# A mixture of softmaxes on one core: one queue for loads and stores, prior read once, last two batches loaded by head

## The chip, the cores and the metric

The kernel runs on one core of one Trainium2 chip. The metric is the device time of one execution in microseconds (us). The profile of one execution has a span about 2 us shorter than the timed value (795.2 against 797.5 us for the kernel before); times quoted "in the span" are from its start. Engines: DVE is the vector engine, ACT the scalar engine, POOL is GpSimd, SP the sync engine, which here only issues DMAs.

## The reference

```
logits (32, 128, 4, 4096) float32, prior (32, 128, 4) float32
p = softmax(prior, last axis)          s = softmax(logits, last axis)
out[b, q, :] = sum over h of p[b, q, h] * s[b, q, h, :]      # (32, 128, 4096) float32
```

The 32 batches are independent. For a batch the 128 positions lie on the 128 partitions; a batch's logits are 8.4 MB, its output 2.1 MB.

## The kernel before

```
lpool bufs=2   # 64 KB per partition each: one batch of logits
epool bufs=4   # bfloat16 exps, 8 KB each
apool bufs=2   # float32 accumulators, 16 KB each
for b in range(B):
    nc.sync.dma_start(out=prior_t, in_=prior[b])             # 128 rows of 16 bytes
    nc.scalar.activation(ep, prior_t, AF.Exp, accum_out=psum)
    nc.vector.reciprocal(rpsum, psum)
    ltile = lpool.tile([P, H, V], FP32, name="ltile")
    if not last:
        nc.sync.dma_start(out=ltile, in_=logits[b])
    acc = apool.tile([P, V], FP32, name="acc")
    for h in range(H):
        ...                     # the last batch is loaded by head, its last head by quarters
        nc.scalar.activation(etile, ltile[:, h], AF.Exp, accum_out=dsum)
        ...                     # coeff = ep[:, h] * rpsum / dsum
        # h == 0: acc = etile * coeff, else: acc = etile * coeff + acc; the very last by quarters
    if not last:
        nc.gpsimd.dma_start(out=out[b], in_=acc)
```

Loads are issued by SP and stores by GpSimd, so they stand in two queues. Below, "load b" and "store b" are the DMAs of batch b, counted from 0. The accumulator of batch b is the one that batch b-2 used: its first accumulation has to wait until store b-2 has landed.

The softmax here doesn't subtract the row's maximum and nothing guards it: scores larger than these inputs give would overflow.

## Time and profile before

| quantity | value | where |
|---|---|---|
| time | 797.48 us (796.5 to 797.49, 3 runs) | runs |
| DVE, ACT busy | 70%, 59% of the span | page |
| DMA busy | 9 tenths or more in 38 of 40 slices | page |
| 64 KB load packet, 16 KB store packet | 2.42 us, 0.611 us | packet records of the trace |
| packets of one DMA engine in sum | 781.7 us | packet records |

A packet is one record of the trace: a piece of a transfer that one DMA engine moves, here 64 KB of a whole load or 16 KB of a store. A transfer has landed when all its completion counts are in.

From the page of the kernel before: the busy time of the engines, the busy share of the DMA engines in 40 slices (in tenths), and the two queues with packets, megabytes and share of 16 engines' span.

```profile
...
DVE 557.5 (70%) x420; ACT 472.1 (59%) x327; POOL 21.1 (3%) x39
...
DMA  9999999999999999999999999999999999999984
...
q1 hardware_dynamic: 10080, 268.51, 78.5%
q0 software_dynamic: 5040, 67.11, 19.8%
...
```

The two queues fill the DMA engines to 98%. The large packets of both run at 27 B/ns; 16 engines of that rate move 432 GB/s. Nobody else is near its limit.

Groups of instructions of the kernel before (line, engine, operation, shapes, count, then busy us in total and mean ns of one, then idle time before them and what ended it), and the DMA issues of prior (count, size each, us from issue to landing).

```profile
...
L78 ACT ACTIVATE etile<-ltile 128x4096 bf16<-128x4096 f32 x127 | 457.6, 3604 | 305.3 <-DMA ltile<-in_logits_dram 305.3
L107 DVE SCALAR_TENSOR_TENSOR acc<-etile,coeff,acc 128x4096 f32<-128x4096 bf16 x95 | 426.1, 4485 | 3.4
...
L105 DVE TENSOR_SCALAR acc<-etile,coeff 128x4096 f32<-128x4096 bf16 x32 | 75.3, 2353 | 1.1
...
prior_t<-in_prior_dram SPq DMA_DIRECT2D x32, 2.0 KB, 34.1
...
```

ACT needs 3.6 us for a head, DVE 2.35 us for the first head of a batch and 4.49 for each other one (SCALAR_TENSOR_TENSOR, "STT" in the prediction). Both fit well into the 24.2 us that the DMA engines need for one batch. ACT's idle time, 305 us, is waiting for loads.

The timeline of the tail (start us, duration us, engine, line, operation, operands; in brackets the idle time before).

```profile
...
746.45 0.53 POOL L116 DMA_DIRECT2D out_dram<-acc  x1 [23.06 <-DVE acc L107]
748.85 3.62 ACT L78 ACTIVATE etile<-ltile 128x4096 bf16<-128x4096 f32 x1 [10.14 <-DMA ltile<-in_logits_dram]
...
753.10 2.35 DVE L105 TENSOR_SCALAR acc<-etile,coeff 128x4096 f32<-128x4096 bf16 x1
...
771.29 2.65 POOL L116 DMA_DIRECT2D out_dram<-acc  x1 [24.31 <-DVE rden L82]
771.48 2.34 DVE L105 TENSOR_SCALAR acc<-etile,coeff 128x4096 f32<-128x4096 bf16 x1
...
789.02 0.53 POOL L103 DMA_DIRECT2D out_dram<-acc  x1 [0.67 <-DVE acc L95]
```

Load 30 lands at 748.7 us, batch 30's first accumulation is at 753.10, batch 31's at 771.48, and DVE works through without a pause of note. It has no idle time before the line at 771.48: store 29, issued at 746.45 in the other queue, was long out of the way.

The issue of load 2, and the window of the start (stretch, its length, then busy us of DVE, ACT and POOL, clock, DMA share, GB/s):

```profile
...
37.58 0.33 SPq L50 DMA_DIRECT2D ltile<-in_logits_dram  x1
...
```

```profile
...
38.00:46.00 8.00, 7.16 (x5) 3.14 (x1) 0.49 (x1) 1.00 0.92 393
...
```

### The profile page before, as it was taken

To read this page: it belongs to the slowest core of one execution; us is meant where nothing else is said; L and a number is where in the kernel's file an instruction comes from. 1 tells how busy PE (TensorE), PEld (TensorE's weight loads), DVE (VectorE), ACT (ScalarE), POOL (GpSimd) and SP (SyncE) were. 2 spreads that over 40 slices of the span, in tenths; PEclk is the share of its full clock that TensorE was granted. 3 is DMA by queue.
4 is the path that set the end of the run, shared out by engine and by line. 5 is a ranking of instruction groups with operands and counts; after the bars stand their busy time and mean duration, and the time that the engine had idled before them with its cause. 6 is when DMAs were issued, how large, how long until landed. Compare 5 with 4: busy or idle time off the path is not lost.

```text
span 795.2 us, 1113 instructions
## 1 busy us (share of the span) xinstructions
DVE 557.5 (70%) x420; ACT 472.1 (59%) x327; POOL 21.1 (3%) x39
## 2 busy tenths in 40 slices
DVE  0686678666687666786666876667866668766696
ACT  0776456765547755567655477545676555775491
POOL 0000000000000000000000000000000000000011
DMA  9999999999999999999999999999999999999984
GB/s 383 452 409 434 406 444 422 437 454 407 452 419 439 439 422 456 401 455 410 450 416 444 445 412 457 404 454 411 458 420 418 457 411 459 407 441 451 401 342 185
DMA packets 15131, 335.70 MB, mean 422 GB/s; under 512 B 5777, under 2 KB 5777, under 8 KB 6801
## 3 DMA queue, kind: packets, MB, share of 16 engines
q1 hardware_dynamic: 10080, 268.51, 78.5%
q0 software_dynamic: 5040, 67.11, 19.8%
q14 instruction: 11, 0.08, 0.0%
HBM read 268.50 MB, written 67.11 MB: 422 GB/s over the span
## 4 chain that ended last, share of the span: by engine, by line
DMA 66%; ACT 22%; issue 7%; DVE 4%; DVEq 0%; ACTq 0%; POOLq 0%; SPq 0%; POOL 0%
DMA ltile<-in_logits_dram 66%; ACT etile L78 22%; DVE acc L107 3%; DVE acc L95 0%; DVE acc L105 0%; DVE coeff L84 0%; DVEq L142 0%; ACTq L78 0%; DVE rden L82 0%; POOLq L142 0%; ACT ep L44 0%; SPq L41 0%; POOL out_dram L103 0%; DVE dsum L75 0%; DVE rpsum L46 0%
## 5 line engine op out<-in xcount | busy, mean ns | idle before, releaser
L78 ACT ACTIVATE etile<-ltile 128x4096 bf16<-128x4096 f32 x127 | 457.6, 3604 | 305.3 <-DMA ltile<-in_logits_dram 305.3
L107 DVE SCALAR_TENSOR_TENSOR acc<-etile,coeff,acc 128x4096 f32<-128x4096 bf16 x95 | 426.1, 4485 | 3.4
L82 DVE RECIPROCAL rden<-dsum 128x1 f32<-128x1 f32 x128 | 20.4, 160 | 220.6 <-ACT etile L78 220.6
L105 DVE TENSOR_SCALAR acc<-etile,coeff 128x4096 f32<-128x4096 bf16 x32 | 75.3, 2353 | 1.1
L116 POOL DMA_DIRECT2D out_dram<-acc x31 | 18.7, 604 | 754.8 <-DVE acc L107 730.5
L84 DVE TENSOR_SCALAR coeff<-ep,rpsum,rden 128x1 f32<-128x1 f32 x128 | 34.9, 273 | 3.5
L78 ACT ACTIVATION_READ_ACCUMULATOR etile<-ltile 128x1 f32 x127 | 23.7, 186 | 0.0
L46 DVE RECIPROCAL rpsum<-psum 128x1 f32<-128x1 f32 x32 | 4.6, 145 | 2.7 <-ACT ep L44 2.7
L44 ACT ACTIVATE ep<-prior_t 128x4 f32<-128x4 f32 x32 | 6.1, 189 | 0.4 <-DMA prior_t<-in_prior_dram 0.4
L44 ACT ACTIVATION_READ_ACCUMULATOR ep<-prior_t 128x1 f32 x32 | 6.0, 187 | 0.0
L95 DVE SCALAR_TENSOR_TENSOR acc<-etile,coeff,acc 128x1024 f32<-128x1024 bf16 x4 | 4.9, 1281 | 0.0
L68 ACT ACTIVATE etile<-ltile 128x1024 bf16<-128x1024 f32 x4 | 4.2, 1042 | 0.0
L103 POOL DMA_DIRECT2D out_dram<-acc x4 | 2.1, 532 | 13.5 <-DVE acc L95 13.5
L44 ACT ACT_TABLE_LOAD x1 | 1.3, 1283 | 0.7 <-PEq L131 0.7
L68 ACT ACTIVATION_READ_ACCUMULATOR etile<-ltile 128x1 f32 x4 | 0.8, 189 | 0.0
L75 DVE TENSOR_REDUCE dsum<-denom 128x1 f32<-128x4 f32 x1 | 0.1, 150 | 0.0
L131 POOL MEMSET const-float32-0.0<- 128x1 f32 x1 | 0.1, 98 | 0.2 <-issue 0.2
L131 POOL MEMSET const-bfloat16-1.0<- 128x1 bf16 x1 | 0.1, 101 | 0.0
L131 POOL MEMSET const-uint8-127<- 128x1 uint8 x1 | 0.1, 99 | 0.0
L131 POOL MEMSET const-float32-1.0<- 128x1 f32 x1 | 0.1, 98 | 0.0
## 6 DMA issues: line engine op xcount, KB each, us to landing
out_dram<-acc POOLq DMA_DIRECT2D x31, 2048.0 KB, 26.1
ltile<-in_logits_dram SPq DMA_DIRECT2D x3, 2048.0 KB, 24.5
ltile<-in_logits_dram SPq DMA_DIRECT2D x4, 512.0 KB, 30.0
out_dram<-acc POOLq DMA_DIRECT2D x4, 512.0 KB, 3.5
prior_t<-in_prior_dram SPq DMA_DIRECT2D x32, 2.0 KB, 34.1
ltile<-in_logits_dram SPq DMA_DIRECT2D x31, 34.4
```

The costliest lines, as they stand in the source:

```text
L44: nc.scalar.activation(ep, prior_t, AF.Exp, accum_out=psum)
L46: nc.vector.reciprocal(rpsum, psum)
L68: nc.scalar.activation(etile[:, c * CW : (c + 1) * CW], ltile[:, h, c * CW : (c + 1) * CW], AF.Exp, accum_out=denom[:, c : c + 1],)
L78: nc.scalar.activation(etile, ltile[:, h], AF.Exp, accum_out=dsum)
L82: nc.vector.reciprocal(rden, dsum)
L84: nc.vector.tensor_scalar(out=coeff, in0=ep[:, h : h + 1], scalar1=rpsum, scalar2=rden, op0=ALU.mult, op1=ALU.mult,)
L95: nc.vector.scalar_tensor_tensor(out=acc[:, cs], in0=etile[:, cs], scalar=coeff, in1=acc[:, cs], op0=ALU.mult, op1=ALU.add,)
L103: nc.gpsimd.dma_start(out=out[b, :, cs], in_=acc[:, cs])
L105: nc.vector.tensor_scalar_mul(out=acc, in0=etile, scalar1=coeff)
L107: nc.vector.scalar_tensor_tensor(out=acc, in0=etile, scalar=coeff, in1=acc, op0=ALU.mult, op1=ALU.add,)
L116: nc.gpsimd.dma_start(out=out[b], in_=acc)
L131: nc = _bacc.Bacc("TRN2", target_bir_lowering=False, num_devices=1)
```

## The change

The intent: take the small packets of prior out of the DMA stream, put loads and stores into one hardware queue in an order fixed by the program, and have the last two batches computed head by head as they arrive. Cut to its core:

```diff
-    epool bufs=4   (bfloat16)
+    epool bufs=2   (float32, the same bytes)
+    def pieces(b):
+        return 1 if b >= B - 2 else H          # heads per load
+    load(0)
+    nc.sync.dma_start(out=pr, in_=prior)       # [32 batches, 128 positions, 4 heads]
+    load(1)
+    ...       # softmax of prior on 32 partitions, 16 transposes of 32x32 to pp[128, H, B]
     for b in range(B):
-        nc.sync.dma_start(out=prior_t, in_=prior[b])
-        nc.scalar.activation(ep, prior_t, AF.Exp, accum_out=psum)
...
+                store(b - 1)       # last batch, last head: the store of batch 30
+                for c in range(NCHUNK):
+                    ...            # accumulate a quarter; after each second one:
+                        store(b, (c - 1) * CW, (c + 1) * CW)
-        if not last:
-            nc.gpsimd.dma_start(out=out[b], in_=acc)
+        if b + 2 < B:
+            load(b + 2)                        # SP
+        if not last and b < B - 2:
+            store(b)                           # SP, after the load
```

The order in the queue is thus load 2, store 0, load 3, store 1, and at the end load 30 (4 pieces), store 28, load 31 (4 pieces), store 29, store 30, two halves of store 31.

More of the change, by code (lines that the diff above doesn't have):

```diff
@@ L9 @@
 FP32 = mybir.dt.float32
-BF16 = mybir.dt.bfloat16
 AF = mybir.ActivationFunctionType
 ALU = mybir.AluOpType
+AX = mybir.AxisListType
 @with_exitstack
@@ L27, with load, store @@
     P = 128
-    assert S == P
+    assert S == P and B == 32
     lpool = ctx.enter_context(tc.tile_pool(name="lpool", bufs=2))
-    epool = ctx.enter_context(tc.tile_pool(name="epool", bufs=4))
+    epool = ctx.enter_context(tc.tile_pool(name="epool", bufs=2))
     apool = ctx.enter_context(tc.tile_pool(name="apool", bufs=2))
     spool = ctx.enter_context(tc.tile_pool(name="spool", bufs=8))
+    cpool = ctx.enter_context(tc.tile_pool(name="cpool", bufs=1))
+    def pieces(b):
+        return 1 if b >= B - 2 else H
+    ltiles = {}
+    def load(b):
+        lt = lpool.tile([P, H, V], FP32, name="ltile")
+        n = pieces(b)
+        for h in range(0, H, n):
+            nc.sync.dma_start(out=lt[:, h : h + n], in_=logits[b, :, h : h + n, :])
+        ltiles[b] = lt
+    accs = {}
+    def store(b, lo=0, hi=V):
+        nc.sync.dma_start(out=out[b, :, lo:hi], in_=accs[b][:, lo:hi])
+    load(0)
+    pr = cpool.tile([B, S, H], FP32, name="pr")
+    nc.sync.dma_start(out=pr, in_=prior)
+    load(1)
+    pmax = cpool.tile([B, S], FP32, name="pmax")
+    nc.vector.reduce_max(pmax, pr, axis=AX.X)
+    pc = cpool.tile([B, S, H], FP32, name="pc")
+    nc.vector.tensor_sub(pc, pr, pmax.unsqueeze(2).to_broadcast([B, S, H]))
+    pe = cpool.tile([B, S, H], FP32, name="pe")
+    nc.scalar.activation(pe, pc, AF.Exp)
+    psum = cpool.tile([B, S], FP32, name="psum")
+    nc.vector.reduce_sum(psum, pe, axis=AX.X)
+    prec = cpool.tile([B, S], FP32, name="prec")
+    nc.vector.reciprocal(prec, psum)
+    pn = cpool.tile([B, H, S], FP32, name="pn")
+    nc.vector.tensor_mul(
+        pn.rearrange("b h s -> b s h"), pe, prec.unsqueeze(2).to_broadcast([B, S, H])
+    )
+    pp = cpool.tile([P, H, B], FP32, name="pp")
+    for t in range(S // 32):
+        for h in range(H):
+            nc.vector.transpose(
+                pp[32 * t : 32 * (t + 1), h, :], pn[:, h, 32 * t : 32 * (t + 1)]
+            )
     NCHUNK = 4
@@ L39 @@
         last = b == B - 1
-        prior_t = spool.tile([P, H], FP32, name="prior_t")
-        nc.sync.dma_start(out=prior_t, in_=prior[b])
-        ep = spool.tile([P, H], FP32, name="ep")
-        psum = spool.tile([P, 1], FP32, name="psum")
-        nc.scalar.activation(ep, prior_t, AF.Exp, accum_out=psum)
-        rpsum = spool.tile([P, 1], FP32, name="rpsum")
-        nc.vector.reciprocal(rpsum, psum)
-        ltile = lpool.tile([P, H, V], FP32, name="ltile")
-        if not last:
-            nc.sync.dma_start(out=ltile, in_=logits[b])
+        lt = ltiles.pop(b)
@@ L52 @@
         acc = apool.tile([P, V], FP32, name="acc")
+        accs[b] = acc
         for h in range(H):
-            if last:
-                if h < H - 1:
-                    nc.sync.dma_start(out=ltile[:, h], in_=logits[b, :, h, :])
-                else:
-                    for c in range(NCHUNK):
-                        nc.sync.dma_start(
-                            out=ltile[:, h, c * CW : (c + 1) * CW],
-                            in_=logits[b, :, h, c * CW : (c + 1) * CW],
-                        )
@@ L64 @@
-            etile = epool.tile([P, V], BF16, name="etile")
-            denom = spool.tile([P, NCHUNK], FP32, name="denom")
-            if last and h == H - 1:
-                for c in range(NCHUNK):
-                    nc.scalar.activation(
-                        etile[:, c * CW : (c + 1) * CW],
-                        ltile[:, h, c * CW : (c + 1) * CW],
-                        AF.Exp,
-                        accum_out=denom[:, c : c + 1],
-                    )
-                dsum = spool.tile([P, 1], FP32, name="dsum")
-                nc.vector.reduce_sum(dsum, denom, axis=mybir.AxisListType.X)
-            else:
-                dsum = spool.tile([P, 1], FP32, name="dsum")
-                nc.scalar.activation(
-                    etile, ltile[:, h], AF.Exp, accum_out=dsum
-                )
+            split = last and h == H - 1
@@ L81 @@
+            et = epool.tile([P, V], FP32, name="etile")
+            dsum = spool.tile([P, 1], FP32, name="dsum")
+            nc.scalar.activation(et, lt[:, h], AF.Exp, accum_out=dsum)
+            coeff = spool.tile([P, 1], FP32, name="coeff")
             rden = spool.tile([P, 1], FP32, name="rden")
             nc.vector.reciprocal(rden, dsum)
-            coeff = spool.tile([P, 1], FP32, name="coeff")
-            nc.vector.tensor_scalar(
-                out=coeff,
-                in0=ep[:, h : h + 1],
-                scalar1=rpsum,
-                scalar2=rden,
-                op0=ALU.mult,
-                op1=ALU.mult,
-            )
@@ L92 @@
-            if last and h == H - 1:
+            nc.vector.tensor_mul(coeff, rden, pp[:, h, b : b + 1])
+            if h == 0:
+                nc.vector.tensor_scalar_mul(out=acc, in0=et, scalar1=coeff)
+            elif not split:
+                nc.vector.scalar_tensor_tensor(
+                    out=acc, in0=et, scalar=coeff, in1=acc, op0=ALU.mult, op1=ALU.add
+                )
+            else:
+                store(b - 1)
                 for c in range(NCHUNK):
@@ L95 @@
                     nc.vector.scalar_tensor_tensor(
-                        out=acc[:, cs],
-                        in0=etile[:, cs],
-                        scalar=coeff,
-                        in1=acc[:, cs],
-                        op0=ALU.mult,
-                        op1=ALU.add,
-                    )
-                    nc.gpsimd.dma_start(out=out[b, :, cs], in_=acc[:, cs])
-            elif h == 0:
-                nc.vector.tensor_scalar_mul(out=acc, in0=etile, scalar1=coeff)
-            else:
-                nc.vector.scalar_tensor_tensor(
-                    out=acc,
-                    in0=etile,
-                    scalar=coeff,
-                    in1=acc,
-                    op0=ALU.mult,
-                    op1=ALU.add,
-                )
-        if not last:
-            nc.gpsimd.dma_start(out=out[b], in_=acc)
+                        out=acc[:, cs], in0=et[:, cs], scalar=coeff, in1=acc[:, cs],
+                        op0=ALU.mult, op1=ALU.add,
+                    )
+                    if c % 2:
+                        store(b, (c - 1) * CW, (c + 1) * CW)
[3 more added lines that the diff above has]
+            store(b)
 _INS = ['logits', 'prior']
```

## The prediction

> **What bounds the kernel now.** The 16 DMA engines, by bytes. The page shows DMA at 9 tenths in 38 of 40 slices, 422 GB/s over the span; DVE is busy 70%, ACT 59%. In the trace's packets a 64 KB load packet takes 2.42 us and a 16 KB store packet 0.611 us: 27 B/ns for loads and stores, alone or mixed. From 3 to 770 us the engines' packets leave no idle time. They sum to 781.6 us per engine, a little overlapped; idle are 2.3 us at the start and about 14 us at the tail. The Trainium skill ("DMA: Bandwidth & Descriptors", section "Issuing engines are not separate DMA queues") says that all issuers share these engines; the trace agrees. One queue instead of two moves no byte faster.
>
> **What the change does.**
> 1. Prior: 4096 packets of 16 B at 9 ns (2.3 us per engine) become 32 rows of 2 KB (about 0.2 us). Fewer DMAs and larger tail pieces save perhaps 0.8 us; the first load starts 0.45 us earlier. All on the critical path: about -3.5 us.
> 2. Float32 exps change no duration (ACT 3.6 us per 4096; STT 4.49; TENSOR_SCALAR 2.35, where the Trainium skill "VectorE: DVE Perf Modes", tier table, gives float32 the 2x mode that this duration shows). Two exp buffers instead of four tie ACT to DVE two heads behind, so a batch's last exp comes about 3 us later: slack in the steady state (the next load is issued some 10 us before its turn).
> 3. Start: prior lands behind load 0 (22.6 us); then a chain of about 7 us (max, sub, exp behind the first large exp, sum, reciprocal, product, 16 transposes) delays the first accumulation. With two exp buffers batch 0's last exp ends near 43 us; load 2 waits for it, while load 1 is through at 40.7. A DMA gap: +3 us.
> 4. Tail, the decisive part. In one queue, store 29 stands behind load 31. Batch 31 accumulates into the buffer that store 29 reads, so its first DVE operation waits until about 6.5 us after load 31 has gone through, though its data came by head. Then DVE needs 2.35 + 3 x 4.9 us and the last half store 2.4 us: the end comes about 30 us after load 31's last packets. Before, it was 22 us, since store 29 shared the engines with load 31. The loads end earlier, at about 765.5 instead of 773, as two stores (9.7 us) now come after them. So the tail gives back what the order saved.
>
> **Sum.** Packets up to load 31 about 760.7 us (loads 621, stores 0 to 28 141.9, less the overlap), start 1.75, gap 3.2, tail 30.4: a span of 796 us against 795.2. Timed: 798 us, range 793 to 804. Faster by over 2% 0.03, within 2% 0.93, slower 0.04.
>
> **What the profile would show.** DMA 9 tenths but for a dip near 41-44 us and an emptier last 25 us; load packets still 2.42 us; DVE's first accumulation of each batch waiting for the store two batches back (about 6 us after the landing, harmless in the middle); batch 31's TENSOR_SCALAR waiting for store 29; the chain's end on DVE and a store; DVE busy near 550 us; 16 transposes under 3 us.
>
> **What would make it wrong.** Idle time at each change from load to store within one queue (64 changes: 0.1 us each is 6 us); a slower packet rate for stores from the hardware queue; batch 31's accumulation not waiting for store 29: then the end comes near 784 us, and without a start gap 781, the limit of "faster".

## The result, and the profile after

800.94 us median (800.46 to 801.67, 4 runs) against 797.49 us (796.5 to 797.68, 4 runs) in the same rounds. The ratio is 1.0051, with a 95% interval of 1.0035 to 1.0067: slower by half a per cent, within the band that counts as the same, and inside the predicted range. All ratios here are the mean time of one kernel's fast runs over the mean of the other's in the same rounds, so they are not quite the ratio of the medians. The kernel before had medians from 795.94 to 797.49 us in four sessions; experiments are therefore compared with each other by their ratios to it, and a difference of two ratios is put into us by multiplying with 797. The intervals of two ratios together leave such a difference uncertain by about 0.002, or 1.6 us.

The same parts of the page of the changed kernel:

```profile
...
DVE 547.0 (68%) x408; ACT 473.1 (59%) x258; POOL 0.2 (0%) x4
...
DMA  9989999999999999999999999999999999999992
...
q1 hardware_dynamic: 10272, 335.61, 97.7%
...
```

One queue now holds all bytes and fills the engines to 97.7%. The last digit of the DMA row has fallen from 4 to 2, and the third is no longer a 9: the engines are idle at the end and once near the start.

The groups of the changed kernel, and the issue of prior:

```profile
...
L94 ACT ACTIVATE etile<-ltile 128x4096 f32<-128x4096 f32 x128 | 462.4, 3613 | 314.1 <-DMA ltile<-in_logits_dram 250.4
L102 DVE SCALAR_TENSOR_TENSOR acc<-etile,coeff,acc 128x4096 f32<-128x4096 f32 x95 | 426.0, 4484 | 3.4
...
L100 DVE TENSOR_SCALAR acc<-etile,coeff 128x4096 f32<-128x4096 f32 x32 | 75.3, 2353 | 29.0 <-DMA out_dram<-acc 29.0
...
pr<-in_prior_dram SPq DMA_DIRECT2D x1, 64.0 KB, 22.0
```

Durations are those of before: float32 exps cost ACT 3.613 instead of 3.604 us and DVE nothing. The Trainium skill, "VectorE: DVE Perf Modes", the perf-mode tier table, gives `tensor_scalar` with float32 the 2x mode. The trace agrees: 4096 elements took 2353 ns, against 4484 ns for SCALAR_TENSOR_TENSOR, and the bfloat16 input before had taken the same 2353 ns. What is new is the end of the TENSOR_SCALAR line: 29.0 us of idle time that a store ended.

**The start.** The window and the issue of load 2 by SP:

```profile
...
38.00:46.00 8.00, 7.86 (x7) 6.06 (x5) 0.00 (x0) 1.00 0.69 262
...
```

```profile
...
43.00 0.33 SPq L45 DMA_DIRECT2D ltile<-in_logits_dram  x1
...
```

The DMA share in this window is 0.69 against 0.92. The packet records give 2.57 us of idle time per DMA engine between 38 and 50 us, and none there before. Load 1 was through, and load 2 was issued only at 43.00 us (before: 37.58). The timeline before it:

```profile
...
23.23 0.67 DVE L60 TENSOR_REDUCE pmax<-pr 32x128 f32<-32x512 f32 x1 [23.23 <-DMA pr<-in_prior_dram]
...
30.04 1.96 DVE L78 STREAM_TRANSPOSE pp<-pn 32x32 f32<-32x32 f32 x16
...
32.23 2.35 DVE L100 TENSOR_SCALAR acc<-etile,coeff 128x4096 f32<-128x4096 f32 x1
...
39.26 3.62 ACT L94 ACTIVATE etile<-ltile 128x4096 f32<-128x4096 f32 x1 [0.87 <-DVE rden L97]
...
```

Prior landed behind load 0, at 23.2 us; its softmax and 16 transposes (1.96 us) were done at 32.0; the first accumulation ran at 32.23. Batch 0's last exp started at 39.26 us, when an exp buffer was free, and load 2 waits for it.

**The tail.** The timeline, and the chain of waits that ended last (start us, us, what):

```profile
...
752.85 2.35 DVE L100 TENSOR_SCALAR acc<-etile,coeff 128x4096 f32<-128x4096 f32 x1 [3.20 <-DMA out_dram<-acc]
...
769.38 3.62 ACT L94 ACTIVATE etile<-ltile 128x4096 f32<-128x4096 f32 x1 [1.08 <-issue]
...
777.23 2.35 DVE L100 TENSOR_SCALAR acc<-etile,coeff 128x4096 f32<-128x4096 f32 x1 [3.75 <-DMA out_dram<-acc]
...
789.19 4.87 DVE L109 SCALAR_TENSOR_TENSOR acc<-etile,coeff,acc 128x1024 f32<-128x1024 f32 x4
```

```profile
...
745.49 31.71 DMA out_dram<-acc
...
777.23 2.36 DVE acc L100
...
```

The list of waits of the changed kernel (us in total, times, longest us):

```profile
...
DVE acc L100 <- DMA out_dram<-acc: 29.0, 30, 3.8
...
```

Load 31's last piece landed at 772.3 us. Two of batch 31's four exps were done by 772.9 us (the second is the line at 769.38); the other two wait for exp buffers, and those for DVE. DVE's first accumulation of batch 31 started at 777.23 us, 0.03 us after store 29 had landed (777.20). Batch 30's (the line at 752.85) had waited for store 28 in the same way. From 777.23 us on it is DVE to 794.1 us and the last half store, which landed at 798.05.

Landings of the last DMAs, from the completion counts in the trace (16 counts per DMA, read here as one from each engine: while those of store 30 come in, from 777.1 to 782.0 us, the packets in flight fall from 10 to none; "lag" is the time from the first to the last count):

```
changed kernel:  load 31 heads 0..3  757.7 762.6 767.5 772.3   lag 5.0
                 store 29 777.2  store 30 782.0  (lag 5.0)   halves of 31: 795.6 798.0  (lag 0.2)
kernel before:   load 31, its four last quarters  769.6 770.8 772.1 773.5   lag 3.1 to 3.3
```

More than one engine is late. Of the 16 counts of load 31's last piece, nine come within 0.7 us and the other seven spread over the rest in the changed kernel; in the kernel before 13 come within 0.7 us and three later.

### The profile page after: what moved, and what is told of

It reads as the page before. It is cut to its first block, busy times and chain, and to the rows that moved or that the text cites. A ratio compares the mean times of both kernels' runs of the same rounds, so it can differ in the third digit from the quotient of the medians.

```text
span 798.9 us, 996 instructions
## 1 busy us (share of the span) xinstructions
DVE 547.0 (68%) x408; ACT 473.1 (59%) x258; POOL 0.2 (0%) x4
## 3 DMA queue, kind: packets, MB, share of 16 engines
q1 hardware_dynamic: 10272, 335.61, 97.7%
## 4 chain that ended last, share of the span: by engine, by line
DMA 63%; DVE 16%; ACT 13%; issue 6%; DVEq 0%; ACTq 0%
DMA ltile<-in_logits_dram 56%; DVE acc L102 13%; ACT etile L94 13%; DMA out_dram<-acc 8%; DVE acc L100 1%; DVE rden L97 1%; DVE coeff L98 1%; DVE acc L109 0%; DVE pp L78 0%; DVEq L144 0%; DVE pn L71 0%; DVE prec L68 0%; DVE psum L66 0%; ACT pe L64 0%; ACTq L94 0%
## 5 line engine op out<-in xcount | busy, mean ns | idle before, releaser
L94 ACT ACTIVATE etile<-ltile 128x4096 f32<-128x4096 f32 x128 | 462.4, 3613 | 314.1 <-DMA ltile<-in_logits_dram 250.4
L102 DVE SCALAR_TENSOR_TENSOR acc<-etile,coeff,acc 128x4096 f32<-128x4096 f32 x95 | 426.0, 4484 | 3.4
L100 DVE TENSOR_SCALAR acc<-etile,coeff 128x4096 f32<-128x4096 f32 x32 | 75.3, 2353 | 29.0 <-DMA out_dram<-acc 29.0
L98 DVE TENSOR_TENSOR coeff<-rden,pp 128x1 f32<-128x1 f32 x128 | 20.4, 159 | 4.4
L60 DVE TENSOR_REDUCE pmax<-pr 32x128 f32<-32x512 f32 x1 | 0.7, 673 | 23.2 <-DMA pr<-in_prior_dram 23.2
L109 DVE SCALAR_TENSOR_TENSOR acc<-etile,coeff,acc 128x1024 f32<-128x1024 f32 x4 | 4.9, 1281 | 0.0
L78 DVE STREAM_TRANSPOSE pp<-pn 32x32 f32<-32x32 f32 x16 | 1.9, 169 | 0.1
```

The lines of the kernel that those rows point to most:

```text
L60: nc.vector.reduce_max(pmax, pr, axis=AX.X)
L78: nc.vector.transpose(pp[32 * t : 32 * (t + 1), h, :], pn[:, h, 32 * t : 32 * (t + 1)])
L94: nc.scalar.activation(et, lt[:, h], AF.Exp, accum_out=dsum)
L98: nc.vector.tensor_mul(coeff, rden, pp[:, h, b : b + 1])
L100: nc.vector.tensor_scalar_mul(out=acc, in0=et, scalar1=coeff)
L102: nc.vector.scalar_tensor_tensor(out=acc, in0=et, scalar=coeff, in1=acc, op0=ALU.mult, op1=ALU.add)
```

## The experiments

My theory: the smaller DMA work is given back by two waits that the change makes, (a) the start gap and (b) batch 31's accumulation standing behind store 29. Rivals: the single queue or hardware stores lower the DMA rate; float32 exps or the two buffers cost throughout; the tail is plain DVE work.

### Four exp buffers again

```diff
-    epool bufs=2, float32
+    epool bufs=4, bfloat16
```

> Changed kernel with four bfloat16 exp buffers in place of two float32 ones (same bytes). My theory: the DMA gap at 41-44 us comes of the two buffers, which tie batch 0's last exp (39.3-42.8 us) to the second accumulation. With four, batch 0's last exp ends near 38.5 us, load 2 is issued before load 1 is through, the gap of 2.6 us goes, the tail stays as it is: about 798.2 us (-2.7). ACTIVATE stays at 3.61 us, TENSOR_SCALAR at 2.35. Rival A (the late prior chain alone makes the gap): the gap stays, 801. Rival B (float32 exps are dearer everywhere): a shorter ACTIVATE or TENSOR_SCALAR, and more than 5 us gained.

796.93 us, ratio 1.0009 (0.9997 to 1.0020): 0.0042 less than the changed kernel, 3.3 us. Load 2's issue and the window:

```profile
...
38.09 0.33 SPq L46 DMA_DIRECT2D ltile<-in_logits_dram  x1
...
```

```profile
...
38.00:46.00 8.00, 7.96 (x7) 3.45 (x2) 0.00 (x0) 1.00 0.91 393
...
```

The gap is gone, load 2 is issued 4.9 us earlier, and ACTIVATE is 3605 ns, TENSOR_SCALAR 2353. So the float32 type costs nothing; the number of buffers does, and only at the start. Rivals A and B fall. The gain cannot be told apart from the 2.6 us of the gap.

### Prior's load first

```diff
-    load(0)
     nc.sync.dma_start(out=pr, in_=prior)
+    load(0)
```

> Changed kernel with prior's load issued before load 0; two float32 exp buffers as they were. My theory: the gap at 41-44 us needs both the two exp buffers and the late prior chain, so either alone cures it. Prior lands near 2.5 us, the first accumulation starts near 27.3 us instead of 32.2, batch 0's last exp ends near 39 us, load 2 is issued about 3.8 us earlier, the gap shrinks from 2.6 us to under 0.5; load 0 starts 0.45 us later. About 798.5 us (797.3 to 799.8). Rival (two buffers alone make the gap): it stays over 2 us, 801.

797.81 us, ratio 1.0018 (1.0004 to 1.0032), 0.0033 or 2.6 us less than the changed kernel. Load 2's issue:

```profile
...
39.15 0.33 SPq L45 DMA_DIRECT2D ltile<-in_logits_dram  x1
...
```

With two float32 buffers still there, the gap is gone too (no idle time in the packet records from 38 to 50 us). The gap needs both causes, and either cure is enough.

### Three accumulators

```diff
-    epool bufs=2 float32, apool bufs=2
+    epool bufs=2 bfloat16, apool bufs=3      # float32 exps would not fit beside the third
```

> Changed kernel with three accumulators (two bfloat16 exp buffers make the room; still two). My theory: batch 31's first accumulation no longer waits for store 29 (777.2 us); it follows its own loads, stores 29 and 30 run while batch 31 is computed, and the end comes about 11 us earlier: about 789.5 us (787 to 792). The gap at 41-44 us stays. Rival (the tail is bounded by DVE work, not by the wait): less than 3 us gained.

790.00 us, ratio 0.9922 (0.9911 to 0.9934): 0.0129 or 10.3 us less than the changed kernel. Its tail (start, us, instruction):

```profile
...
746.63 2.35 DVE L101 TENSOR_SCALAR acc<-etile,coeff 128x4096 f32<-128x4096 bf16 x1
...
764.91 2.35 DVE L101 TENSOR_SCALAR acc<-etile,coeff 128x4096 f32<-128x4096 bf16 x1
...
778.40 4.87 DVE L110 SCALAR_TENSOR_TENSOR acc<-etile,coeff,acc 128x1024 f32<-128x1024 bf16 x4
780.91 2.72 SPq L52 DMA_DIRECT2D out_dram<-acc  x2
```

Batch 31's first accumulation is at 764.91 us, 12.3 us earlier, and with no wait; load 31 itself landed at 773.2, no earlier than in the changed kernel. The start gap stayed (2.07 us). This measures the waits for stores 28 and 29 together: batch 30's first accumulation, at 746.63 us, is already 6.2 us earlier, and no run separates the two. The halves of the last store are now issued at 780.91 and 783.30 us, while store 30 lands at 783.0: the engine that is last has no pause left, and it lands the last half at 787.80. But the other engines, which had stood idle until DVE released the first half, land theirs at 787.10 to 787.26. So the packets of the slowest engine set the end, with DVE's chain only 0.5 us behind them.

### The last two batches loaded whole

```diff
-        return 1 if b >= B - 2 else H
+        return H
```

> Changed kernel with the last two batches loaded whole, as all others. My theory: the loads by head buy nothing here, since batch 31's accumulation waits for store 29, which lands 4.9 us after the whole load and one exp (3.6 us) fits before: 801 us, +-0.7. Rival (loads by head shorten the tail): 5 to 12 us slower.

801.12 us, ratio 1.0062 (1.0050 to 1.0074), not told apart from the changed kernel (1.0035 to 1.0067). In the changed kernel the loads by head buy nothing, as expected: the data waits for the accumulator.

### Stores in a queue of their own

```diff
-        nc.sync.dma_start(out=out[b, :, lo:hi], ...)
+        nc.gpsimd.dma_start(out=out[b, :, lo:hi], ...)
```

> Changed kernel with all stores issued from GpSimd, a second queue, nothing else changed. My theory: store 29 shares the engines with load 31 and lands near 757 us instead of 777, batch 31's accumulation follows its loads, which come 5 to 10 us later (777 to 782): the end 4 to 10 us earlier, about 793 us (790 to 797). The gap at 41-44 us stays. Rival (the queue does not matter, tail is DVE work): 801. Rival B (stores from the hardware queue slow the packets): load packets' mean falls from 2434 ns, and the lag of the slowest of the 16 engines falls below 5 us.

796.69 us, ratio 1.0007 (0.9994 to 1.0020): 0.0044 or 3.5 us less than the changed kernel, which cannot be told apart from the lower end of the 4 to 10 that were expected. Tail:

```profile
...
764.82 2.35 DVE L100 TENSOR_SCALAR acc<-etile,coeff 128x4096 f32<-128x4096 f32 x1
...
778.10 3.62 ACT L94 ACTIVATE etile<-ltile 128x4096 f32<-128x4096 f32 x1 [4.80 <-DMA ltile<-in_logits_dram]
...
787.41 0.53 POOL L51 DMA_DIRECT2D out_dram<-acc  x1 [1.86 <-DVE acc L109]
```

Batch 31's first accumulation is early, as expected (764.82 us, no wait). But load 31's last piece, which now shared the engines with store 30, was there only at 778.1, and after it came an exp, an accumulation and the stores with nothing left to move meanwhile: 16 us to the end. Load packets' mean was 2433 ns against 2434 in the changed kernel, so hardware stores do not slow the packets. That half of rival B falls; its other half, a lag under 5 us, came true (4.0 us at load 31's last piece, 2.2 at store 30).

### Stores 28 and 29 before loads 30 and 31

```diff
+        if b in (B - 4, B - 3): store(b)
         if b + 2 < B:
             load(b + 2)
-        if not last and b < B - 2:
+        if not last and b < B - 4:
             store(b)
```

> Changed kernel with stores 28 and 29 issued before loads 30 and 31 in the one queue, nothing else changed. My theory: load 31 lands one store (4.9 us) later, near 777, but batch 31's accumulation waits for its own data alone; end about 7.5 us earlier: about 793.3 us (791.5 to 795.5). Rival (the wait was not decisive, the tail is DVE work): 800 or more.

793.17 us, ratio 0.9961 (0.9948 to 0.9973): 0.0090 or 7.2 us less than the changed kernel. These are the waits for stores 28 and 29 cured by order alone, with no buffer added. The list of waits (us in total, times, longest us):

```profile
...
DVE acc L100 <- DMA out_dram<-acc: 22.1, 28, 1.4
...
```

In the changed kernel the longest such wait was 3.8 us and is now 1.4. Load 31 landed at 777.1, 4.8 us later, as expected. A kernel cured in this way has one store more in front of load 31, which lands 3.9 us later than with three accumulators, and one fewer to fill the time behind it; that this is why it stays behind that kernel was not tested.

### All stores before the loads

```diff
-        if b + 2 < B:
-            load(b + 2)
         if not last and b < B - 2:
             store(b)
+        if b + 2 < B:
+            load(b + 2)
```

> Changed kernel with store b issued before load b+2 for all batches. A batch's accumulation ends about 21 us after its landing when it need not wait for an older store, the engines need 24.2 us per batch, so the store should just come in time. My theory: no waits of the accumulation for stores; like the swapped tail, about 793 us (790 to 797), slack under 3 us per batch. Rival (load first in the queue is needed to keep the engines fed): 10 us or more slower than the changed kernel, with DMA idle in the middle.

799.42 us, ratio 1.0037 (1.0023 to 1.0050), which is neither my 793 nor the rival's 811. The list of waits:

```profile
...
DVE acc L100 <- DMA out_dram<-acc: 0.8, 1, 0.8
...
```

The waits for stores are gone (0.8 us in all against 29.0). The DMA engines stand idle for 1.9 us on average between 50 and 740 us, where the changed kernel has nothing, so the rival had the idle time right and its size wrong. What I had missed is the price of "just in time", which is more than this idle time. In the middle, groups of 16 KB packets take up to 1.2 us instead of 0.611, just where a queue that is nearly empty passes from a load to a store; their mean rises from 611 to 633 ns, 7 us per engine in sum, and load 31 lands at 783.2 instead of 777.1 in the run above. That these are packets waiting for their successors to be issued fits their places in the trace, but was not tested. So load-first is the right order for the middle, where a load must stand ready, and the wrong one for the last two batches.

### Kernel before, prior read once

```diff
-        nc.sync.dma_start(out=prior_t, in_=prior[b])
+        prior_t = pp[:, b, :]      # one load before the loop, copied and transposed 32x32
```

> Kernel before with prior read once and transposed on the chip, its small exps and everything else as they were. My theory: 4096 packets of 16 B at 9 ns are 2.3 us per engine, and some 500 completion packets fall away (0.3 us), all within the bound; 32 packets of 2 KB take 0.2 us. About 2.3 us faster than before: ratio 0.997 (0.9955 to 0.9985). Rival (small packets hide between the large ones): ratio 1.000.

792.76 us against 796.80, ratio 0.9955 (0.9943 to 0.9967): 3.6 us, at the far edge of what was expected. The packets of one engine sum to 779.3 instead of 781.7 us, which is the 2.4 us of the theory. The rest lies in the lag of the slowest engine: at load 30 it was 2.3 us instead of 4.3, and load 30 landed at 744.5 instead of 748.7. Whether the small packets made that lag, or one run differs from another in it, stays open.

### Kernel before, batch 30 by head too

```diff
-        if not last: load logits[b] whole
+        if b < B - 2: load logits[b] whole
+        elif not last: load logits[b] by head
```

> Kernel before with batch 30 loaded by head too, stores on their own queue as they were. My theory: the loads by head do pay where no store stands in front: batch 30's first accumulation starts near 746.7 us instead of 753.1, and with it the whole tail, which is a chain of DVE: about 6 us faster, ratio 0.9925 (0.990 to 0.996). Rival (the tail hangs on the landing of load 31, not on batch 30): ratio 1.000.

794.03 us, ratio 0.9968 (0.9954 to 0.9983): 2.5 us faster, under the 6 expected and just outside the range given, though its interval reaches into it.

```profile
...
747.33 2.35 DVE L108 TENSOR_SCALAR acc<-etile,coeff 128x4096 f32<-128x4096 bf16 x1
...
777.60 1.06 ACT L71 ACTIVATE etile<-ltile 128x1024 bf16<-128x1024 f32 x1 [2.55 <-DMA ltile<-in_logits_dram]
...
781.93 4.87 DVE L98 SCALAR_TENSOR_TENSOR acc<-etile,coeff,acc 128x1024 f32<-128x1024 bf16 x4
...
```

Batch 30's first accumulation is at 747.33 us, 5.8 us earlier than before, as foreseen. But load 31's second quarter was there only at 777.60 us (770.8 before), with lags up to 9.7 us among the engines, and the tail then hung on it. Loads by head are worth something with two queues, less than the DVE chain alone suggests.

### Both cures together

```diff
-    epool bufs=2 float32, apool bufs=2, load(0) before prior
+    epool bufs=3 bfloat16, apool bufs=3, prior before load(0)
     # pr, pc and pe of the prior softmax share one tile, so that all fits
```

> Changed kernel with three accumulators, three bfloat16 exp buffers, prior's load first and its small tiles reused in place. My theory: both losses go; the slowest of the 16 engines works without a pause from load 0 to the last store: about 786.8 us (785.5 to 788.5), DMA idle at 38-50 us none. Rival (the two losses are one, as the engines' lag absorbs the start gap): as with three accumulators alone, 790.

786.65 us (785.61 to 786.97, 4 runs) against 795.94 us, ratio 0.9877 (0.9863 to 0.9891): 1.2% faster than before and 0.0174 or 13.9 us faster than the changed kernel; results correct. Window and tail:

```profile
...
38.00:46.00 8.00, 6.85 (x4) 3.46 (x1) 0.00 (x0) 1.00 0.91 393
...
```

```profile
...
773.71 4.87 DVE L108 SCALAR_TENSOR_TENSOR acc<-etile,coeff,acc 128x1024 f32<-128x1024 bf16 x4
776.21 2.73 SPq L52 DMA_DIRECT2D out_dram<-acc  x2
```

The start window is back at 0.91. The last half stores are issued before store 30 has landed (779.2 us), and the last lands at 784.0. The rival, that the two losses are one, falls: 3.6 us (0.0045) lie between this kernel and the one with three accumulators alone. The edit also has a third exp buffer, which unties ACT from DVE in the tail; no run separates its share from the start gap's. What bounds it now is the engine that is last: its lag was 5.6 us at store 30, and it lands the last half store 1.5 us after the other engines.

## Why the prediction was right

1. *What bounds the kernel.* Right. The Trainium skill, "DMA: Bandwidth & Descriptors", section "Issuing engines are not separate DMA queues", says all issuers' DMAs run on the same engines. Here the 64 KB packets took 2418 ns in the median in every kernel, and 16 KB packets 611 ns with stores in either queue.
2. *Prior, -3.5 us.* Direction right; alone in the kernel before it gave 3.6 us, but of another make-up: 2.4 us by packets and the rest by a smaller lag.
3. *Float32 exps cost nothing; two buffers are slack in the middle.* Right: same durations, and four buffers gained 3.3 us in all, the start gap and little else.
4. *Start gap of 3.2 us at 41 to 44 us.* Right: 2.57 us of idle time, caused by both the late prior and the two buffers, either of which cures it.
5. *Tail: batch 31's accumulation waits for store 29.* Right, and the decisive part: 10.3 us with a third accumulator, 7.2 by order alone, nothing by loading the batches whole. The first two cures take away batch 30's wait for store 28 too.
6. *Sizes.* The predicted span was 796, measured 798.9. "6.5 us after load 31 has gone through" at 765.5 puts store 29's landing at 772.0; it landed at 777.2. This term was mis-sized by 5.2 us. The sum was made for the average engine and its mean packet of the kernel before. A landing needs the slowest of 16, and at store 29 it was 3.5 us behind the average of the 16; the mean 64 KB packet, 2434 ns against 2425, adds 2.3 us over the 240 packets of the average engine. The 6.5 us held only 1.6 of this, beside the 4.9 of the store itself; with the start gap 0.6 smaller this estimate explains about 3.6 of the 5.2 us, and the other 1.6 stay open. The loads' end "at about 765.5 instead of 773" has the same fault: 765.5 is the sum for the average engine, 773 was the slowest engine's landing. From slowest to slowest, load 31 landed at 772.3 instead of 773.5, so the order saved 1.2 us there and not 7.5. In the other direction, from store 29's landing to the end it took 21.7 us instead of 24. Of these 2.3 us, 1.5 are the end of the program after the last landing: 0.8 us with the hardware queue, where I had carried over the 2.3 of the kernel before (the prediction does not write this out). That the span came within 3 us of 796 is in part luck: the two errors have opposite signs.
7. *"Then the end comes near 784 us, and without a start gap 781".* Too low: 790.0 and 786.65. It is probably the same lag, since at store 30 the slowest engine was 4.6 and 4.0 us behind the average of the 16, which is the larger part of what is missing; but no run takes the lag away, so this is argued and not shown.

What stays open is why some engines fall behind. The lag grows in steps, from 0.5 us at 42 us to 5.0 at 578 us in the changed kernel, and the packet records do not name the engines.

So the change moved little because about 3 us of start gap and 10 of waiting ate what it won: with both removed, and a third exp buffer, the same order of loads and stores is 13.9 us faster.

## What to carry to other kernels

When loads and stores go into one in-order queue, look at which buffer each store frees and what waits for that buffer: behind the last loads a store that stands in the wrong place puts the whole remaining computation after the DMA work instead of beside it. One more accumulator, or the last stores moved ahead of the last loads, settles it here (10.3 and 7.2 us). Stores that still wait behind the last load may be useful as work for the DMA engines while the last piece is computed; this fits the runs but was not tested apart. For a bound by DMA, count the slowest engine and not the mean, and look at the first two buffers and the last two apart from the steady state: here the middle of the kernel was DMA work without a pause in all versions but one.

## What the Trainium skill lacked or had wrong

- "DMA: Bandwidth & Descriptors", the section on latency and other measured facts, says that two DMA engines are usually slower and guesses a cause that only the software queue has. Here engines fell behind without that queue too: where all bytes went through the hardware queue the lag was 5.0 us at load 31 in the changed kernel and 5.6 to 6.1 us at store 30 in the two fastest versions, with seven of 16 counts late and not two. With GpSimd's stores it was 3.3 us at load 31 in the kernel before, but up to 9.7 us with batch 30 loaded by head, so neither kind of queue is free of it. In the run whose queue ran nearly dry every batch it was 0.3 to 0.7 us over loads 30 and 31. Which engines are late the records do not say.
- The same page's measured table gives 341 GB/s for a 1 MB transfer. That is for loads issued from GpSimd; queued one behind another in the hardware queue, the two 1 MB stores at the end of the changed kernel landed 2.46 us apart (426 GB/s), and the 2 MB heads and stores before them 4.84 to 4.90 us apart (428 to 433 GB/s).
- The same page has nothing on a queue that is filled just in time: 16 KB packets of up to 1.2 us instead of 0.611 at the change from load to store, about 7 us in all.
- No page that I looked up has the end of a program after the last landing: 0.8 to 0.9 us where all stores were on the hardware queue, 2.2 to 2.6 us where they were issued from GpSimd.
- "VectorE: DVE Perf Modes", the section on transpose paths, gives one time for a large tile; 16 float32 transposes of 32x32 took 1.96 us here in a row, 169 ns in the mean for one, as they overlap.
